# A planner that counts packets and holds transfers back: one change to the plan of the DMA queue

## The chip, the core and the metric

The kernel runs on one core of a Trainium2 chip. A core has five engines with an instruction queue each: PE (TensorE, matrix products), DVE (VectorE), ACT (ScalarE), POOL (GpSimd) and SP (SyncE). In this kernel SP does nothing but issue transfers between the chip's memory (DRAM in the code) and the core's own memory; 16 DMA engines then move the bytes. Each queue is worked off strictly in its order: an instruction that waits holds up everything behind it on its engine. The metric is the device time of one execution in microseconds (us); less is better.

## The reference, cut to what matters

One layer of a hybrid encoder, for 2048 positions of width 1024. The input is normalised and projected once, and the columns of the projection go to two groups of heads:

```python
h = rms_norm(x, norm_w[l])
proj = h @ w_in[l]
dn = gated_deltanet_bidir(dn_q, dn_k, dn_v, dn_beta, dn_decay, ...)   # 4 heads of 128, both directions
dn = rms_norm(dn, dn_out_norm_w[l]) * silu(dn_z)
sw = windowed_gqa_with_sinks(sw_q, sw_k, sw_v, ...)                   # 8 query heads of 64, |i-j| <= 128
sw = sw * silu(sw_z)
x = x + concatenate([dn, sw]) @ w_out[l]
```

The first group (DeltaNet) applies a short convolution to q, k and v. It then cuts the positions into chunks, and for each chunk solves a small triangular system. Finally it carries a state from chunk to chunk, once forward and once backward. The second group is attention in blocks of 128 queries over a band of 384 keys.

## The kernel before, in words

**Stages.** Phase A works in two halves of 1024 positions. It loads x and the weights, splits both into a high and a low part, and does three matmuls for each product (lines 190 to 192 and 201 to 203). It runs the convolution (line 241) and the windowed attention in between. What later stages need goes out to DRAM: k and q of a head to `kq_d`, v to `v_d`, the gates to `zdn_d` and `zsw_d`, the attention's result to `mix_sw`.

Phase B takes the four DeltaNet heads in turn. For each head, `pre_front` loads four pieces of k, q (tile `kq`, line 654) and v (`vt`, 656) and a decay table (`dc`, 664), and writes the triangular matrices to DRAM (`m_d`, 708). `solve` reads their diagonal blocks back (`X` and `L`, 731 and 732), inverts them on DVE in 31 steps, and writes the result to DRAM (`x_d`, 746). `invert` reads it back in another layout (`xc`, 757) and builds the whole inverses with matmuls on PE (772). `scan` then goes through 16 chunks in both directions; each step loads `kqc` (810), which has four buffers for a direction, and ends in `post` (mix of the normalised output with the gate, 864 to 882).

While one head is in its scan, the next one is in `pre_front`, `solve` and `invert`. Between them lie 32 units of the output projection of the attention part (`sw_units`, lines 568 to 604). Each unit loads `mxs` (587) and often `zcs` (590), splits it (594, 595), loads a piece of x (`xrs`, 597), multiplies (600 to 602), adds on DVE (603) and stores a part of the sum (`part`, 604). At the end `out_dn` adds the DeltaNet part and writes the output (554 to 566).

**What sets the order.** No order is written out by hand. `set_order` (line 936) takes all instructions, works out which depends on which, gives each a duration, and plans them against a model of the five engines. `plan` (line 1161) is a list scheduler: the engine that can start first takes, of the instructions whose inputs are there, the one with the highest priority. It is run forward and backward in turn, 12 rounds (line 1224), each pass giving the other its priorities; the best of the last five forward plans is kept. The chosen order is then fixed for each of the five queues (line 1235). So the planned times never reach the chip: only the five orders do.

**The model of a transfer.** SP is busy for 500 ns with each issue (line 1084). The moving is done by one resource, `bus`, that takes one transfer after the other; `move[k]` (line 1114) is how long it holds it, and a transfer's data counts as there after its start on the bus plus the issue, a lag of 2400 ns (line 929) and its `move`. Before the change `move` is the bytes over 300 bytes per ns, whatever their layout, and SP may issue the next transfer however many are waiting for `bus` (lines 1205 to 1207). The first 14 loads have a fixed order, and no other transfer is issued before the last of them (lines 1069 to 1078).

Of the kernel before, what the change touches and what calls it, by code (L numbers as in the profile page):

```python
# [13 lines left out]
DRAM = bass.MemoryType.DRAM  # L14
# [921 lines left out]
def set_order(tc):  # L936


    insts, boundaries = [], []
# [7 lines left out]
    tiles = {x.name: x for x in tc.tiles}  # L947

    def aps(l):
        return [a.bass_ap for a in l if hasattr(a, "bass_ap")]  # L950

    def size(a):
        r = 1
        for _, c in list(a.ap)[1:]:
            r *= c
        return r

    def box(a, shape):
        stride = [1] * len(shape)
        for d in range(len(shape) - 2, -1, -1):  # L960
            stride[d] = stride[d + 1] * shape[d + 1]
        lo, off = [], a.offset
        for s in stride:
            lo.append(off // s)
            off %= s
        hi = list(lo)
        for step, count in a.ap:
            if step > 0 and count > 1:
                d = next(d for d, s in enumerate(stride) if s <= step)
                hi[d] += -(-(count - 1) * step // stride[d])  # L970
        for d in range(len(shape) - 1, 0, -1):
            if hi[d] >= shape[d]:
                hi[d - 1] += hi[d] // shape[d]
                lo[d], hi[d] = 0, shape[d] - 1
        return lo, hi
# [13 lines left out]
    for k, (i, eng) in enumerate(insts):  # L989
        touched = [(a, False) for a in aps(i.ins)] + [(a, True) for a in aps(i.outs)]  # L990
        for a, w in touched:
            name = a.tensor.name
            if name not in tiles:
                continue
            x = tiles[name]
            psum = "PSUM" in str(x.space)
            b = box(a, list(x.shape))
            used.setdefault(name, []).append(k)
            past = hist.setdefault(name, [])
            for k2, e2, w2, b2 in past:  # L1000
                if (w or w2) and (
                    (psum and (e2 == "PE") != (eng == "PE"))
                    or all(p <= s and r <= q for p, q, r, s in list(zip(b[0], b[1], b2[0], b2[1]))[1:])
                ):
                    edge(k2, k, w2)
            if psum and eng != "PE" and past and past[-1][1] != "PE" and past[-1][0] != k:
                if past[-1][1] == eng:
                    started[past[-1][0]].append(k)
                else:
                    edge(past[-1][0], k)  # L1010
            past.append((k, eng, w, b))
# [34 lines left out]
    for x in sorted((x for x in tc.tiles if x.tag in home and x.name in used), key=lambda x: used[x.name][0]):  # L1046
        name, bufs = home[x.tag]
        users.setdefault(name, []).extend(used[x.name])
        k = used[x.name][0]
# [6 lines left out]
        r = ring.setdefault(x.tag, [])  # L1056
# [18 lines left out]
    for x in used:  # L1075
        k = used[x][0]
# [32 lines left out]
    move, late = [0.0] * total, [0.0] * total  # L1109
    nxt, prv = [[] for _ in range(total)], [[] for _ in range(total)]  # L1110
    for k in range(total):
        if eng[k] == "SP":
            a = aps(insts[k][0].outs)[0]
            move[k] = a.ap[0][1] * size(a) * 4 / 300
            spread = [x.ap[0][0] == 0 for x in aps(insts[k][0].ins)]
            late[k] = 2000 * any(spread)
        lag = LAG[eng[k]] + move[k] + late[k] if k < n else 0
        if eng[k] == "PE" and not insts[k][0].is_transpose and "float32r" not in str(insts[k][0].ins[0].dtype):
            lag += 40
        if eng[k] == "Activation" and len(aps(insts[k][0].outs)) > 1:  # L1120
            lag += 90
        for s in succ[k]:
            if eng[s] == eng[k] != "SP":
                nxt[k].append((s, SAME[eng[k]] * ((k, s) in wrote)))
            else:
                nxt[k].append((s, lag))
        for s in started[k] if k < n else ():
            nxt[k].append((s, None))
        for s, d in nxt[k]:
            prv[s].append((k, d))  # L1130
# [30 lines left out]
    def plan(order, forward):  # L1161
        to, back = (nxt, prv) if forward else (prv, nxt)
        left, at = [len(x) for x in back], [0.0] * total
        later, ready = {e: [] for e in ENGINES}, {e: [] for e in ENGINES}
        free, queue = dict.fromkeys(ENGINES, 0.0), {e: [] for e in ENGINES}
        begin, bus, held = [0.0] * total, 0.0, 0.0

        def release(k, t):
            todo = [(k, t)]
            while todo:  # L1170
                k, t = todo.pop()
                for s, d in to[k]:
                    if d is not None:
                        at[s] = max(at[s], t + dur[k] + slow[k] + d)
                    else:
                        at[s] = max(at[s], t if forward else t + dur[k] + slow[k] - dur[s] - slow[s])
                    left[s] -= 1
                    if left[s]:
                        continue
                    if eng[s]:  # L1180
                        heapq.heappush(later[eng[s]], (at[s], s))
                    else:
                        begin[s] = at[s]
                        todo.append((s, at[s]))

        for k in range(total):
            if not back[k] and eng[k]:
                heapq.heappush(later[eng[k]], (0.0, k))
            elif not back[k]:
                release(k, 0.0)  # L1190
        for _ in range(n):
            t, e = min(
                (free[e] if ready[e] else max(free[e], later[e][0][0]), e) for e in ENGINES if ready[e] or later[e]
            )
            while later[e] and later[e][0][0] <= t:
                k = heapq.heappop(later[e])[1]
                heapq.heappush(ready[e], (order[k], k))
            k = heapq.heappop(ready[e])[1]
            queue[e].append(k)
            if k in port:  # L1200
                t = max(t, held)
                held = t + dur[k]
            begin[k] = t
            free[e] = t + dur[k] + slow[k]
            if e == "SP":
                release(k, max(t, bus))
                bus = max(t, bus) + move[k]
            else:
                release(k, t)
        end = max(free.values())  # L1210
        return end, begin, queue
# [9 lines left out]
    for k in reversed(topo):  # L1221
        rank[k] = max([dur[k]] + [rank[s] if d is None else rank[s] + dur[k] + d for s, d in nxt[k]])
    now, best = plan([-r for r in rank], True), None
    for i in range(12):
        if i < 8:
            stretch(*now[1:])
        back = plan([-(b + d) for b, d in zip(now[1], dur)], False)
        now = plan([-(b + d) for b, d in zip(back[1], dur)], True)
        if i >= 7 and (best is None or now[0] < best[0]):
            best = now  # L1230
# [64 lines left out]
```

## Time and profile before

| | before |
|---|---|
| time, median of 3 runs | 1291.93 us (1291.03 to 1295.85) |
| the profiled execution's own time | 1291.8 us |
| its span, first to last instruction | 1290.0 us |
| mean granted TensorE clock | 0.988 |
| instructions | 22619 |
| bytes moved, mean rate | 205.36 MB, 159 GB/s |

The profile is of one execution. Its page gives busy times for each engine, the span in slices, the DMA queues, the chain of work that ended last (followed back from the last instruction, at each step to what released it), and the costliest groups of instructions. Further views of the trace give the busy time of each engine in chosen stretches, the transfers of a stretch with their median time from issue to landing, and the queue of one engine in order of time. "DMA share" is the mean busy share of the 16 DMA engines; slightly above 1 is possible, since packets are counted by the stretch in which they begin.

### The profile page before, as it was taken

How to read it: one execution, taken by the hardware profiler on the slowest of the kernel's cores; microseconds unless marked ns; L12 is line 12 of the kernel's file. 1: busy time of each engine (PE TensorE's matmuls, PEld its weight loads, DVE VectorE, ACT ScalarE, POOL GpSimd, SP SyncE). 2: the span in 40 equal slices, each digit the busy share in tenths (PEclk: the TensorE clock that was granted, in tenths of full speed). 3: DMA queues.
4: the chain of work that ended last, by engine and by line, in shares of the span. 5: the costliest groups of instructions: out<-in, count | busy, mean ns of one | idle time of the engine just before them, and what ended most of it. 6: DMA issues, size and time to landing. Idle time of an engine off the chain costs nothing.

```text
span 1290.0 us, 22619 instructions
## 1 busy us (share of the span) xinstructions
PE 1231.0 (95%) x7162; PEld 1058.8 (82%) x7162; DVE 903.9 (70%) x2266; ACT 718.4 (56%) x2121; POOL 509.8 (40%) x876
## 2 busy tenths in 40 slices
PE   6999989999999999999999997999799899999998
PEld 6998778888889998888888886788688689898876
DVE  4422388999975689999986474689579869656433
ACT  5422254776744577777664325768657845675310
POOL 2230053757612297665320104833582482640000
PEclk9999999999999999999999997999999999999999
DMA  7442243322544433422127736966965875644765
GB/s 260 148 131 84 84 163 121 116 83 90 156 149 145 127 104 103 150 90 75 71 93 234 219 100 204 254 176 200 282 162 174 267 204 172 196 152 133 253 236 207
DMA packets 225511, 205.36 MB, mean 159 GB/s; under 512 B 48496, under 2 KB 175088, under 8 KB 225392
## 3 DMA queue, kind: packets, MB, share of 16 engines
q1 hardware_dynamic: 225392, 203.92, 50.9%
q8 instruction: 57, 0.93, 0.3%
q14 instruction: 62, 0.51, 0.1%
HBM read 138.79 MB, written 65.08 MB: 158 GB/s over the span
## 4 chain that ended last, share of the span: by engine, by line
PE 68%; DVE 13%; issue 6%; DMA 6%; ACT 4%; POOL 3%; SPq 0%; DVEq 0%; POOLq 0%; ACTq 0%
PE pf_c L190 5%; PE pf_c L191 5%; PE pf_c L192 5%; PE pf_z L190 4%; PE pf_z L191 4%; PE pf_z L192 4%; PE pi L772 3%; PE pt L364 3%; DVE acc L241 2%; PE pq_q L201 2%; PE pq_q L202 2%; PE pq_q L203 2%; PE pcd L563 2%; PE pcd L564 2%; PE pcd L562 2%
## 5 line engine op out<-in xcount | busy, mean ns | idle before, releaser
L190 PE MATMUL pf_c<-xhi,wh_c 128*128 128x512 f32 x384 | 151.2, 406 | 3.2 <-DVE acc L241 3.2
L241 DVE SCALAR_TENSOR_TENSOR acc<-pf_c,cw,acc 128x512 f32<-128x512 f32 (+2 forms) x192 | 140.0, 742 | 17.0 <-ACT acc L237 16.1
L191 PE MATMUL pf_c<-xlo,wh_c 128*128 128x512 f32 x384 | 151.0, 404 | 0.0
L192 PE MATMUL pf_c<-xhi,wl_c 128*128 128x512 f32 x384 | 149.8, 404 | 0.0
L359 POOL TENSOR_SCALAR pr<-pr,st 128x384 f32<-128x384 f32 (+1 forms) x128 | 84.8, 679 | 73.2 <-DVE st L357 49.9
L192 PE MATMUL pf_z<-xhi,wl_z 128*128 128x512 f32 x256 | 90.8, 401 | 0.0
L191 PE MATMUL pf_z<-xlo,wh_z 128*128 128x512 f32 x256 | 90.8, 399 | 0.0
L190 PE MATMUL pf_z<-xhi,wh_z 128*128 128x512 f32 x256 | 89.8, 400 | 0.0
L190 PEld LDWEIGHTS pf_c<-xhi,wh_c 128*128 128x128 f32 x384 | 72.7, 190 | 16.9 <-DVE acc L241 3.6
L350 ACT ACTIVATE pr<-pr,st 128x384 f32<-128x384 f32 (+1 forms) x128 | 76.1, 596 | 16.4 <-DVE st L349 14.3
L191 PEld LDWEIGHTS pf_c<-xlo,wh_c 128*128 128x128 f32 x384 | 72.6, 190 | 13.7
L192 PEld LDWEIGHTS pf_c<-xhi,wl_c 128*128 128x128 f32 x384 | 72.4, 189 | 13.8
L368 ACT ACTIVATE ph<-pt 128x512 fp32r<-128x512 f32 x92 | 53.7, 594 | 46.9 <-PE pt L364 41.3
L345 DVE CUSTOM_DVE_ANT_0 pr<-s,mask,sink 128x384 f32<-128x384 f32 (+1 forms) x128 | 72.7, 592 | 4.8 <-PE pt L364 2.5
L364 PE MATMUL pt<-ident,pr 128*128 128x128 f32 x368 | 71.5, 275 | 1.5 <-POOL pr L359 1.4
L826 ACT ACTIVATE yk<-py,ck 128x128 f32<-128x128 f32 x120 | 43.8, 365 | 48.4 <-PE py L821 47.2
L684 POOL TENSOR_TENSOR nk<-ssk,pw 128x4 f32<-128x4 f32 x16 | 16.9, 1059 | 131.0 <-DVE ssk L683 95.0
L703 DVE SCALAR_TENSOR_TENSOR ma<-gh,bp,dc 128x256 f32<-128x256 f32 x128 | 55.0, 476 | 19.4 <-PE gh L694 15.2
L369 DVE TENSOR_TENSOR pl<-pt,ph 128x512 fp32r<-128x512 f32 x92 | 62.0, 683 | 6.9 <-ACT ph L368 6.6
L364 PEld LDWEIGHTS pt<-ident,pr 128*128 128x128 f32 x368 | 48.1, 140 | 16.8 <-POOL pr L359 4.1
L202 PE MATMUL pq_q<-wh_q,xlo 128*128 128x256 f32 x256 | 61.5, 283 | 0.0
L201 PE MATMUL pq_q<-wh_q,xhi 128*128 128x256 f32 x256 | 61.1, 285 | 0.0
(253 smaller groups left out, 3798.4 us busy)
## 6 DMA issues: line engine op xcount, KB each, us to landing
kqc<-kq_d SPq DMA_DIRECT2D x120, 128.0 KB, 2.9
ws_c<-wt SPq DMA_DIRECT2D x48, 256.0 KB, 3.4
xr<-x SPq DMA_DIRECT2D x16, 512.0 KB, 5.3
ws_z<-wt SPq DMA_DIRECT2D x32, 256.0 KB, 3.6
kq<-kq_d SPq DMA_DIRECT2D x16, 512.0 KB, 5.4
m_d<-ma SPq DMA_DIRECT2D x32, 256.0 KB, 5.2
mxs<-mix_sw SPq DMA_DIRECT2D x32, 256.0 KB, 3.6
xrs<-x SPq DMA_DIRECT2D x32, 256.0 KB, 3.5
```

The source lines that it names most:

```text
L190: T.matmul(ps, hi[:, k, cs], xhi[b][:, k], start=(k == 0), stop=False)
L191: T.matmul(ps, hi[:, k, cs], xlo[b][:, k], start=False, stop=False)
L192: T.matmul(ps, lo[:, k, cs], xhi[b][:, k], start=False, stop=(k == KC - 1))
L201: T.matmul(ps[:, :n], xh, hi[:, k, :n], start=(k == 0), stop=False)
L202: T.matmul(ps[:, :n], xl, hi[:, k, :n], start=False, stop=False)
L241: V.scalar_tensor_tensor(av, ps[:, lo:], cw[:, i, k : k + 1], av, ALU.mult, ALU.add)
L345: V.tensor_tensor_reduce(pr[j][:, :n], ps[:, :n], mask[:, lo * P : hi * P], 1.0, sink[:, hh : hh + 1], ALU.add, ALU.max, accum_out=mx[:, j ...
L350: A.activation(pr[j][:, :n], pr[j][:, :n], AF.Exp, bias=nm[:, j : j + 1], accum_out=den[:, j : j + 1])
L359: G.tensor_scalar(pr[j][:, :n], pr[j][:, :n], den[:, j : j + 1], 1.0, ALU.mult, ALU.mult)
L364: T.transpose(pt[:, j], pr[j][:, (kb - lo) * P : (kb - lo + 1) * P], ident)
L369: V.tensor_tensor(pl, ptf, ph.bitcast(F32), ALU.subtract)
L703: V.scalar_tensor_tensor(ma[d, c4][:, c], gh[:, k], bp[:, d, cc : cc + 1], gms[d][:, c : c + 1].to_broadcast([P, 2, P]), ALU.mult, ALU.mult,)
```

## The change

Only the planner's model of a transfer is edited. The instructions, tiles and transfers are those of before; the order in each of the five queues is planned anew.

```diff
+    def run(a):
+        inside = a.tensor.name in tiles and "DRAM" not in str(tiles[a.tensor.name].space)
+        r = 1
+        for step, c in reversed(list(a.ap)[1:] if inside else list(a.ap)):
+            if step != r:
+                break
+            r *= c
+        return min(r, 2048)
+
...
         if eng[k] == "SP":
             a = aps(insts[k][0].outs)[0]
-            move[k] = a.ap[0][1] * size(a) * 4 / 300
+            count = a.ap[0][1] * size(a)
+            piece = min(run(x) for x in aps(insts[k][0].ins) + [a])
+            move[k] = count / piece * (8 + 0.148 * piece) / 16
...
             if e == "SP":
                 release(k, max(t, bus))
                 bus = max(t, bus) + move[k]
+                free[e] = max(free[e], bus - 1000)
             else:
```

`run` gives how many numbers lie in one unbroken piece of a transfer's source or target (within a partition, for a tile of the core's memory), at most 2048. The smaller of the two is the transfer's packet. `move` becomes the number of packets times 8 ns plus 0.148 ns for each 4-byte number, divided by 16 engines. The last added line keeps SP from its next issue until no more than 1000 ns of planned moving is waiting. Both hold in the forward and in the backward passes.

## The prediction

> **What bounds the kernel now.** The page comes first: busy times, the DMA queue, then the shares of the chain that ended last.
>
> ```profile
> PE 1231.0 (95%) x7162; PEld 1058.8 (82%) x7162; DVE 903.9 (70%) x2266; ACT 718.4 (56%) x2121; POOL 509.8 (40%) x876
> q1 hardware_dynamic: 225392, 203.92, 50.9%
> PE 68%; DVE 13%; issue 6%; DMA 6%; ACT 4%; POOL 3%; SPq 0%; DVEq 0%; POOLq 0%; ACTq 0%
> ```
>
> PE is the bound: 1231.0 of 1290.0 us. A new order of the same instructions can only win back idle time, 1290.0 - 1231.0 = 59.0 us, or lose more. DMA engines are half busy on average, but an average over stages hides where they are full. So next I read the busy times by stage, and then by the stretches where DMA fills up (engines in the order PE, PEld, DVE, ACT, POOL, then clock, DMA share, GB/s).
>
> ```profile
> 0.00:50.00 50.00, 38.56 (x267) 36.39 (x268) 25.59 (x42) 28.06 (x61) 15.06 (x38) 0.97 0.72 242
> 50.00:750.00 700.00, 692.21 (x3805) 589.38 (x3804) 515.85 (x1211) 397.11 (x965) 290.98 (x433) 1.00 0.39 122
> 750.00:1195.00 445.00, 410.23 (x2703) 360.99 (x2702) 327.44 (x956) 277.31 (x1055) 202.12 (x405) 0.97 0.65 193
> 1195.00:1290.00 95.00, 90.02 (x394) 72.02 (x392) 35.03 (x60) 15.95 (x43) 1.64 (x1) 1.00 0.68 232
> ```
>
> ```profile
> 785.00:815.00 30.00, 21.50 (x102) 16.79 (x101) 16.21 (x39) 20.55 (x93) 19.05 (x38) 0.72 0.92 262
> 835.00:850.00 15.00, 12.76 (x91) 11.54 (x90) 8.27 (x20) 11.48 (x39) 11.26 (x20) 1.00 0.90 243
> 890.00:930.00 40.00, 30.81 (x180) 24.74 (x179) 31.35 (x95) 28.56 (x124) 19.30 (x28) 0.96 0.87 256
> 1000.00:1050.00 50.00, 43.70 (x262) 36.02 (x261) 36.12 (x107) 35.49 (x147) 29.90 (x63) 0.97 0.88 254
> sum 135.00, PE 108.77 PEld 89.08 DVE 91.94 ACT 96.07 POOL 79.51; mean PE 27.19 PEld 22.27 DVE 22.99 ACT 24.02 POOL 19.88
> ```
>
> PE's idle time is 11.4 us in the opening, 7.8 us in the 700 us of the rest of phase A, 34.8 us in the scans, 5.0 us at the end. Of the 34.8, 135.00 - 108.77 = 26.2 us lie in four stretches in which the DMA share is 0.87 to 0.92. That is where an order of transfers can matter. Little of this idle time names DMA directly, though. In the list of waits the one wait of PE for a transfer in phase B is this:
>
> ```profile
> PE tr L674 <- DMA kq<-kq_d: 1.6, 1, 1.6
> PE tro L878 <- ACT oacc L875: 6.4, 4, 3.9
> ```
>
> The second row is why: PE mostly waits for other engines. The link to DMA is one step further back, in the chain of work in order of time (start, us, what):
>
> ```profile
> 911.26 6.80 DMA x_d<-X
> ...
> 922.67 4.65 DMA xc<-x_d
> ...
> 933.78 5.85 DMA xrs<-x
> ...
> 939.66 0.04 DVE xrs L603
> ...
> 940.26 0.35 DVE r L814
> ...
> 940.66 0.49 PE py L821 x2
> ```
>
> A load of x (`xrs`) arrives, DVE adds it, and only then does DVE reach the scan's `r`, for which PE waits. A late transfer of a filling unit stops the scan through DVE's fixed order.
>
> **The change, part by part.** It adds and removes no instruction on any queue. It does two things to the plan.
>
> *The count.* For 512-byte packets (128 numbers: kqc, dc, m_d, zcs) the old price of one is 128 x 4 / 300 x 16 = 27.3 ns, the new one 8 + 0.148 x 128 = 26.9 ns: no change. For 2 KB packets (mxs, xrs, vt, kq) it falls from 109.2 to 83.8 ns, so 256 KB goes from 874 to 670 ns of bus. For 128-byte packets (X, L, xc) it rises from 6.8 to 12.7 ns, X and L from 874 to 1630 ns each. Over the whole queue the old plan books 203.92 MB / 300 = 680 us; the new one, from the row of q1, (225392 x 8 + 50.98 million x 0.148) / 16 = 584 us. The profile has 50.9% of 1290.0 = 657 us. The new sum is 11% too short, the old one 3.5% too long. By itself I price the count at nothing; bounds are in the rival below.
>
> *The limit.* SP now stands still in the plan while over 1 us of moving waits. With 500 ns for an issue and 670 ns for a 256 KB transfer, the backlog grows by 170 ns each, by 840 ns for kq (1340 ns). So it acts only in bursts. In the full stretches there are bursts. Here are medians from issue to landing, over the whole run, then for 890 to 940 us:
>
> ```profile
> kqc<-kq_d SPq DMA_DIRECT2D x120, 128.0 KB, 2.9
> ...
> mxs<-mix_sw SPq DMA_DIRECT2D x32, 256.0 KB, 3.6
> xrs<-x SPq DMA_DIRECT2D x32, 256.0 KB, 3.5
> ...
> x_d<-X SPq DMA_DIRECT2D x4, 512.0 KB, 4.4
> ```
>
> ```profile
> q1 hardware_dynamic: 20104, 13.10, 88.9%
> ...
> kqc<-kq_d SPq DMA_DIRECT2D x8, 128.0 KB, 5.3
> ...
> mxs<-mix_sw SPq DMA_DIRECT2D x3, 256.0 KB, 5.6
> x_d<-X SPq DMA_DIRECT2D x1, 512.0 KB, 6.8
> ...
> xrs<-x SPq DMA_DIRECT2D x2, 256.0 KB, 5.1
> ```
>
> The excess is queueing: x_d 2.4, mxs 2.0, xrs 1.6, kqc 2.4 us. With at most 1 us allowed to wait, a newcomer finds between 0 and 1 us, 0.5 on average (an estimate). Kept excess 0.5, so x_d gains 1.9, mxs 1.5, xrs 1.1: 4.5 us for this stretch. These three I count one after the other: x_d opens the round trip to the next head's inverses, mxs feeds PE in the meantime, and xrs stands ahead of the scan on DVE, as the chain shows. kqc I count as nothing, covered by its four buffers; without that cover it would add up to 1.9. The same for the other two stretches, first 785 to 815, then 1000 to 1050:
>
> ```profile
> q1 hardware_dynamic: 10994, 7.82, 91.4%
> ...
> mxs<-mix_sw SPq DMA_DIRECT2D x2, 256.0 KB, 5.9
> ...
> xrs<-x SPq DMA_DIRECT2D x1, 256.0 KB, 5.2
> ```
>
> ```profile
> q1 hardware_dynamic: 20750, 12.62, 87.0%
> ...
> mxs<-mix_sw SPq DMA_DIRECT2D x5, 256.0 KB, 4.4
> xrs<-x SPq DMA_DIRECT2D x5, 256.0 KB, 3.9
> ...
> x_d<-X SPq DMA_DIRECT2D x1, 512.0 KB, 5.4
> ```
>
> At 785: mxs 2.3 - 0.5 = 1.8, xrs 1.7 - 0.5 = 1.2, together 3.0. At 1000: x_d 1.0 - 0.5 = 0.5, mxs 0.8 - 0.5 = 0.3, xrs nothing, together 0.8. The sum is 4.5 + 3.0 + 0.8 = 8.3 us. Bounds: with the full 1 us left waiting, 3.0 + 2.0 + 0 = 5.0; with all excess gone, 6.0 + 4.0 + 2.2 = 12.2. What is late next is PE's wait for ACT and DVE in the same places, so nothing beyond the 26.2 us of idle time can follow.
>
> *The rest of the run.* In the opening, the first 14 loads keep their order, so I put nothing. In the rest of phase A a DMA share of 0.39 leaves little to hold back and PE idles 7.8 us: nothing, between a gain of 4 and a loss of 4 (half its idle time either way, a guess at what a fresh order does). At the end, with no other stage beside it, nothing.
>
> The profiled execution is 1291.8 us (span 1290.0 and 1.8 around it), 0.1 below the median. **1291.8 - 8.3 = 1283.5 us.**
>
> One row speaks against holding back: SP's own queue shows that the chip already does.
>
> ```profile
> 936.55 3.80 SPq L732 DMA_DIRECT2D L<-m_d  x1
> ```
>
> An issue planned at 500 ns took 3.80 us while the queue was full, so a plan that stops SP there is nearer the truth. The Trainium skill, "DMA: Bandwidth & Descriptors", section "Rules for kernel authors", says the opposite of holding back: issue a transfer early and wait for it late, so that its fixed cost is hidden. No run shown here tells the two apart. By that rule the time would be that of the first rival, 1300.2 us; by the rows, 1283.5.
>
> **The rivals.**
>
> *Held back and priced too low: slower.* With the limit, a transfer that nobody needs soon is issued only when the planned bus is nearly free, and the planned bus is too fast. From the three q1 rows the new plan books 23.6, 40.3 and 39.6 us of bus in the three stretches (8 ns for a packet, 0.148 for each number, over 16); the old books 26.1, 43.7 and 42.1; the shares of 30, 50 and 50 us measure 27.4, 44.4 and 43.5. The shortfall grows from 3.4 to 11.8 us, by 8.4. Its place is the pieces that feed `pre_front` (kq, vt, dc), each with other engines' fixed orders behind it. If those arrive later by the shortfall, with nothing left between landing and use, the time is 1291.8 + 8.4 = 1300.2 us, 1303.6 with all 11.8. It decides once the planned slack of a load is below about 4 us, one stretch's shortfall. For it: the count is too low. Against it: old orders had landings of 5 to 7 us where the plan had about 4, and PE named DMA for 1.6 us only.
>
> *The limit hardly acts: same.* If SP is held by waits for producers more than by moving, its order stays, and only small re-orderings remain: 1291.8 us, within 4 us. For it: bursts must be long to build up 1 us. Against it: the full shares and the 3.80 us issue.
>
> *More than the excess.* If a better order of transfers lets the scans run on, up to all 26.2 us: 1265.6. Against it: most waits there name ACT and DVE.
>
> **How the numbers follow.** The forecast (1279.6 to 1286.8) has 0.40, the slower rival 0.34, no effect 0.19, the large gain 0.07. A measurement can tell about 0.5% from no change, 6.5 us: below 1285.5 is faster, above 1298.4 slower. Of the forecast 0.33 lies below 1285.5 and 0.07 above; of the slower rival 0.31 lies above 1298.4 and 0.03 below; no effect gives 0.15 same and 0.02 to each side. So faster 0.33 + 0.07 + 0.02 = 0.42, same 0.07 + 0.03 + 0.15 = 0.25, slower 0.33. The range takes in the forecast, part of the large gain, and the slower rival with its whole shortfall: 1272 to 1304. The forecast's own range is 1279.6 to 1286.8.
>
> **What would show it.** Right: landings of x_d, mxs and xrs in the full stretches near 4.5 us, and idle time of PE there down from 26.2 to about 18 us. The slower rival: new waits of PE, ACT or POOL for kq, vt or dc, or for what these feed, at the start of a head. No effect: the same medians. I am wrong altogether if phase A, which I put at nothing, moves by more than 4 us, or if the landings shorten and PE's idle time stays.

## The result and the profile after

The changed kernel takes 1299.67 us (median of 5 runs, 1298.75 to 1302.58) against 1294.21 us for before in the same comparison (5 runs, 1291.03 to 1295.85). The ratio is 1.0052 with an interval of 1.0038 to 1.0066: slower by half a per cent, where 0.6% faster was forecast. The profiled execution took 1299.67 us (span 1297.9). The one of before, 1291.8, lies at the low end of its runs, so the two profiles differ by 7.9 us where the medians differ by 5.5; a few us in a comparison of single profiles are the execution, not the kernel.

The page of after, the same three lines as for before:

```profile
PE 1234.0 (95%) x7162; PEld 1059.9 (82%) x7162; DVE 901.4 (69%) x2266; ACT 718.2 (55%) x2121; POOL 509.0 (39%) x876
q1 hardware_dynamic: 225392, 203.92, 50.7%
PE 72%; DMA 8%; DVE 6%; ACT 5%; POOL 5%; issue 3%; SPq 1%; DVEq 0%; POOLq 0%; ACTq 0%
```

Packets and bytes are the same to the last one, and so are the instruction counts of the engines. What grew is PE's idle time, from 59.0 to 1297.9 - 1234.0 = 63.9 us, and its busy time, by 3.0 us. The latter can be the clock: the opening below ran at 0.93 of it, against 0.97. By stage (engines PE, PEld, DVE, ACT, POOL, then clock, DMA share, GB/s):

```profile
0.00:50.00 50.00, 37.51 (x258) 35.46 (x258) 24.49 (x41) 28.94 (x61) 14.86 (x36) 0.93 0.70 242
50.00:750.00 700.00, 694.27 (x3813) 588.84 (x3813) 514.74 (x1219) 394.69 (x964) 293.79 (x436) 1.00 0.39 122
750.00:1195.00 445.00, 406.04 (x2662) 358.31 (x2660) 320.35 (x930) 273.24 (x1043) 198.73 (x403) 0.97 0.64 187
1195.00:1297.90 102.90, 96.14 (x432) 77.31 (x432) 41.78 (x79) 21.34 (x54) 1.64 (x1) 1.00 0.70 238
```

Fixed stretches mix what was late with what was slow. Two marks cut the run at nearly the same work in every kernel: the last matmul of the gates' projection (`pf_z`, end of phase A's products) and the first of the last output stage (`pcd`). At the first mark PE has started 4217 or 4218 of its 7162 matmuls in every kernel of this document. The view of a tile gives the first and last start of its instructions. Before:

```profile
L192 PE MATMUL pf_z<-xhi,wl_z x256: 387/393/585, 91.9 to 783.2; 128*128 128x512 f32 x128
```

```profile
L562 PE MATMUL pcd<-wohd,mhd x128: 387/389/496, 1194.9 to 1285.5; 128*128 128x512 f32 x128
```

After:

```profile
L192 PE MATMUL pf_z<-xhi,wl_z x256: 388/393/581, 93.7 to 783.2; 128*128 128x512 f32 x128
```

```profile
L562 PE MATMUL pcd<-wohd,mhd x128: 387/389/497, 1202.6 to 1293.4; 128*128 128x512 f32 x128
```

Both reach the first mark at 783.2 us. From there to the second, which I call the scans, before needs 1194.9 - 783.2 = 411.7 us, after 1202.6 - 783.2 = 419.4. The last stage is as long in both (90.6 and 90.8). **The whole loss between these two profiles, 7.7 us, is in the scans.** Here are the engines between the marks, before and then after:

```profile
783.20:1194.90 411.70, 376.93 (x2555) 333.80 (x2553) 301.88 (x887) 270.85 (x1036) 201.22 (x403) 0.97 0.68 201
```

```profile
783.20:1202.60 419.40, 378.43 (x2550) 335.97 (x2548) 303.07 (x886) 271.57 (x1035) 198.73 (x403) 0.97 0.68 197
```

PE's idle time there grows from 411.70 - 376.93 = 34.8 to 419.40 - 378.43 = 41.0 us, so 6.2 of the 7.7 us are waits. A third mark says when they come: PE's first product in the scan of the third head (`py` from `vs`), before and after:

```profile
L821 PE MATMUL py<-vs,ma x4: 272/274/275, 1042.2 to 1045.1; 128*128 128x128 f32 x4
```

```profile
L821 PE MATMUL py<-vs,ma x4: 273/275/275, 1048.4 to 1049.9; 128*128 128x128 f32 x4
```

From the first mark that is 259.0 and 265.2 us: 6.2 us are lost by then, while the first two heads are in their scans and the next ones are prepared.

Now the rows on which the forecast rested. The four full stretches of after:

```profile
785.00:815.00 30.00, 20.56 (x99) 17.13 (x98) 16.58 (x44) 21.75 (x96) 18.73 (x36) 0.77 0.94 269
835.00:850.00 15.00, 14.30 (x99) 12.70 (x98) 9.09 (x26) 12.09 (x40) 12.42 (x21) 1.00 0.75 185
890.00:930.00 40.00, 31.87 (x191) 26.00 (x190) 30.20 (x91) 28.40 (x125) 18.57 (x34) 0.96 0.90 260
1000.00:1050.00 50.00, 42.19 (x244) 34.15 (x245) 35.37 (x106) 34.01 (x148) 26.03 (x56) 0.97 0.83 237
sum 135.00, PE 108.92 PEld 89.97 DVE 91.23 ACT 96.24 POOL 75.75; mean PE 27.23 PEld 22.49 DVE 22.81 ACT 24.06 POOL 18.94
```

Idle time of PE there is 135.00 - 108.92 = 26.1 us; it was 26.2. So the idle time that the scans gained shows outside the four stretches: 41.0 - 26.1 = 14.9 us, where it was 34.8 - 26.2 = 8.6 (as far as fixed stretches can tell, since the work shifts by some us). And the transfers of 890 to 940 us, median us from issue to landing in the last column:

```profile
q1 hardware_dynamic: 20083, 12.75, 90.7%
...
kqc<-kq_d SPq DMA_DIRECT2D x8, 128.0 KB, 5.5
...
x_d<-X SPq DMA_DIRECT2D x1, 512.0 KB, 6.7
mxs<-mix_sw SPq DMA_DIRECT2D x2, 256.0 KB, 3.8
xrs<-x SPq DMA_DIRECT2D x2, 256.0 KB, 5.6
```

Only mxs lands sooner (5.6 before). x_d stays (6.8), xrs and kqc are later (5.1 and 5.3). The other two stretches, 785 to 815 and 1000 to 1050:

```profile
mxs<-mix_sw SPq DMA_DIRECT2D x2, 256.0 KB, 5.2
...
xrs<-x SPq DMA_DIRECT2D x1, 256.0 KB, 7.3
```

```profile
xrs<-x SPq DMA_DIRECT2D x4, 256.0 KB, 3.7
...
mxs<-mix_sw SPq DMA_DIRECT2D x3, 256.0 KB, 3.6
...
x_d<-X SPq DMA_DIRECT2D x1, 512.0 KB, 5.4
```

All eight changes together: (-0.1 - 1.8 + 0.5) + (-0.7 + 2.1) + (-0.2 - 0.8 + 0.0) = -1.0 us, where 8.3 were forecast. In SP's queue in order of time an issue still stands behind the one before it:

```profile
935.41 4.44 SPq L732 DMA_DIRECT2D L<-m_d  x1
```

It took 4.44 us, right behind the load of `X` (3.80 in the same place before). For the first head, where the same load came 4 us after that of `X`, it took 0.59 us in before. Nothing of the limit is in the code that reaches the chip: the five orders are, and the limit has shaped them and nothing else.

### The profile page after: what moved, and what is told of

Its sections match the earlier page's. It is cut to its first block, busy times and chain, and to the rows that moved or that the text cites. A ratio compares the mean times of both kernels' runs of the same rounds, so it can differ in the third digit from the quotient of the medians.

```text
span 1297.9 us, 22582 instructions
## 1 busy us (share of the span) xinstructions
PE 1234.0 (95%) x7162; PEld 1059.9 (82%) x7162; DVE 901.4 (69%) x2266; ACT 718.2 (55%) x2121; POOL 509.0 (39%) x876
## 3 DMA queue, kind: packets, MB, share of 16 engines
q1 hardware_dynamic: 225392, 203.92, 50.7%
## 4 chain that ended last, share of the span: by engine, by line
PE 72%; DMA 8%; DVE 6%; ACT 5%; POOL 5%; issue 3%; SPq 1%; DVEq 0%; POOLq 0%; ACTq 0%
PE pf_c L190 6%; PE pf_c L192 5%; PE pf_c L191 5%; PE pf_z L190 4%; PE pf_z L191 4%; PE pf_z L192 4%; PE pi L772 3%; PE pt L364 3%; PE pq_q L201 2%; PE pq_q L202 2%; PE pq_q L203 2%; PE pcd L562 2%; PE pcd L563 2%; PE pcd L564 2%; DMA kq<-kq_d 2%
## 5 line engine op out<-in xcount | busy, mean ns | idle before, releaser
L241 DVE SCALAR_TENSOR_TENSOR acc<-pf_c,cw,acc 128x512 f32<-128x512 f32 (+1 forms) x192 | 140.5, 742 | 10.1 <-ACT acc L237 7.8
L190 PE MATMUL pf_z<-xhi,wh_z 128*128 128x512 f32 x256 | 87.1, 402 | 0.0
L191 PE MATMUL pf_z<-xlo,wh_z 128*128 128x512 f32 x256 | 86.0, 398 | 0.0
L192 PE MATMUL pf_z<-xhi,wl_z 128*128 128x512 f32 x256 | 85.9, 399 | 0.0
## 6 DMA issues: line engine op xcount, KB each, us to landing
ws_c<-wt SPq DMA_DIRECT2D x48, 256.0 KB, 3.2
ws_z<-wt SPq DMA_DIRECT2D x32, 256.0 KB, 3.8
m_d<-ma SPq DMA_DIRECT2D x32, 256.0 KB, 5.1
mxs<-mix_sw SPq DMA_DIRECT2D x32, 256.0 KB, 3.3
xrs<-x SPq DMA_DIRECT2D x32, 256.0 KB, 3.5
```

The costliest lines, as they stand in the source:

```text
L190: T.matmul(ps, hi[:, k, cs], xhi[b][:, k], start=(k == 0), stop=False)
L191: T.matmul(ps, hi[:, k, cs], xlo[b][:, k], start=False, stop=False)
L192: T.matmul(ps, lo[:, k, cs], xhi[b][:, k], start=False, stop=(k == KC - 1))
L241: V.scalar_tensor_tensor(av, ps[:, lo:], cw[:, i, k : k + 1], av, ALU.mult, ALU.add)
```

## The experiments

Theories at the start: **A**, the first rival, the new price of a transfer is too low. **B**, the limit holds loads back too long. **C**, any new plan of so many instructions lands somewhere within a few tenths of a per cent, whatever the edit says. Later came **D**: the limit gains in phase A and loses in the scans. Each result is the ratio to before, with its interval. The table at the end of this section gives the two parts of each profiled execution, cut at the marks above.

**The two parts of the change alone, and two controls.**

```diff
# count_only: the changed kernel without
-                free[e] = max(free[e], bus - 1000)
# limit_only: the changed kernel with the old price
-            move[k] = count / piece * (8 + 0.148 * piece) / 16
+            move[k] = count * 4 / 300
# rate_301, rate_299: the kernel before with
-            move[k] = a.ap[0][1] * size(a) * 4 / 300
+            move[k] = a.ap[0][1] * size(a) * 4 / 301     # and 299
```

> The new price of a transfer (packets counted) without the limit on SP; before as the base is 1294. Theory A (the new price books too little bus, 584 us against a measured 657, and so the plan counts on loads too early): the loss is the price's, so slower by 0.4 to 0.8%, 1299 to 1304 us, with the loss again at the changes of head. Theory B (the limit holds loads back too long): without the limit the loss is gone, 1289 to 1295 us. Theory C (any new plan of these 22,600 instructions lands somewhere within about 1% of the old, whatever the edit says): anything from 1288 to 1306 us, and the stages in which it gains or loses are not those of the full change.

> The limit of 1000 ns on SP with the old price (bytes over 300). Theory A: the old price books 680 us, more than is measured, so nothing is counted on too early and the limit is free to help or to do nothing: 1283 to 1294 us. Theory B: the old price is higher for most transfers, so the limit acts more often, and the loss is as large as that of the full change or larger: 1300 to 1306 us. Theory C: anything from 1288 to 1306 us, without the pattern of the full change.

> The kernel before with 301 instead of 300 bytes per ns in the planner, no other edit: 0.3% less for the moving of each transfer, a few ns. Theories A and B: nothing that matters is changed, so 1291 to 1297 us (within 0.2% of before). Theory C: the plan is as new as that of the full change, so it differs from before by 0.2 to 0.8%, to either side.

> The kernel before with 299 instead of 300 bytes per ns in the planner, no other edit. Theories A and B: 1291 to 1297 us, as with 301. Theory C: differs from before by 0.2 to 0.8%, to either side, and not by the mirror image of what 301 gives.

Measured: count_only 1.0003 (0.9990 to 1.0017), limit_only 0.9997 (0.9979 to 1.0015), rate_301 1.0009 (0.9996 to 1.0022), rate_299 0.9966 (0.9953 to 0.9979). Neither part alone costs anything, so A and B fall as they stood. And a constant changed by 0.3% moves the time by 0.34% in one case. Compared place by place in the traces, by operation, tiles and shapes, rate_301 has another matmul than before in 4416 of the 7162 places of PE's order and limit_only in 3893: in these plans a constant moved by 0.3% changes the order as much as the limit does. C was the likeliest by now, but the profiles of limit_only and of the full change agreed in one respect. Here is limit_only at the two marks:

```profile
L192 PE MATMUL pf_z<-xhi,wl_z x256: 387/393/585, 89.2 to 779.1; 128*128 128x512 f32 x128
```

```profile
L562 PE MATMUL pcd<-wohd,mhd x128: 388/389/501, 1199.8 to 1290.5; 128*128 128x512 f32 x128
```

It is 4.1 us ahead at the first mark, and needs 420.7 us for the scans, 9.0 more than before. Its total is even because a gain and a loss cancel.

**The limit in one phase only, and the full change with a hair's difference.**

```diff
# lim_A and lim_B: limit_only, with the limit by phase
+    cut = min(used[x][0] for x in used if x.startswith("kq0_"))
...
-                free[e] = max(free[e], bus - 1000)
+                if k < cut:        # lim_B: k >= cut
+                    free[e] = max(free[e], bus - 1000)
# lim_990: the changed kernel with bus - 990; num_1485: with 0.1485 * piece
```

> Old price, with the limit on SP only for the transfers of phase A (those recorded before the first load of pre_front); before as the base is 1295. Both plans with the limit (the full change and the limit alone) were 3 to 5 us ahead of before at 400 us and lost 8 to 9 us between 784 us and the end, the plans without it lost nothing there. Theory D (the limit helps in phase A and hurts in the scans): ahead by 4 us at 784 us and no loss behind it, so 1288 to 1292 us, faster by 0.2 to 0.5%. Theory C (only a new plan's luck): the gain at 784 us is anywhere from -6 to +5 us and the total anywhere from 1288 to 1303 us.

> Old price, with the limit only for the transfers of phase B. Theory D: even with before at 784 us, and 7 to 10 us lost by the end of the scans, most of it in the scan of the second head, so 1301 to 1305 us. Theory C: anywhere from 1288 to 1303 us, and where it loses or gains is another place than in the full change.

> The full change with 990 instead of 1000 ns in the limit, nothing else: the same idea in every respect, with a plan that differs in part. Theory A, B and D (the loss comes from what the change says): 1299 to 1303 us, as the full change. Theory C: the full change was an unlucky plan, and this one lies elsewhere by 0.2 to 0.6%, more likely lower: 1290 to 1299 us.

> The full change with 0.1485 instead of 0.148 ns for a number, nothing else. Theory A, B and D: 1299 to 1303 us, as the full change. Theory C: elsewhere by 0.2 to 0.6%, more likely lower: 1290 to 1299 us.

Measured: lim_A 0.9963 (0.9943 to 0.9983), lim_B 1.0044 (1.0031 to 1.0058), lim_990 1.0052 (1.0035 to 1.0069), num_1485 1.0043 (1.0028 to 1.0058). All four times came as D has it. The place that was named for lim_B did not: of its 7.4 us more in the scans than before, 4.8 are lost before the second head's scan begins. C, for the full change, falls: two neighbours, whose orders of PE differ from its own in 1510 and 3451 places, lose as much. The marks of lim_A:

```profile
L192 PE MATMUL pf_z<-xhi,wl_z x256: 387/393/585, 89.1 to 779.1; 128*128 128x512 f32 x128
```

```profile
L562 PE MATMUL pcd<-wohd,mhd x128: 388/389/501, 1189.3 to 1279.9; 128*128 128x512 f32 x128
```

and of lim_B:

```profile
L192 PE MATMUL pf_z<-xhi,wl_z x256: 387/393/585, 92.2 to 785.0; 128*128 128x512 f32 x128
```

```profile
L562 PE MATMUL pcd<-wohd,mhd x128: 388/389/501, 1204.1 to 1294.7; 128*128 128x512 f32 x128
```

lim_A is as far ahead at 779.1 as limit_only and needs 410.2 us for the scans; lim_B gains nothing in phase A and needs 419.1. And -0.37% + 0.44% is about the 0 of limit_only.

**The parts put together, and SP's order by itself.**

```diff
# count_lim_A: the changed kernel with the limit for k < cut only
# lim_A_301: lim_A with 301 instead of 300
# sp_of_lim: the plan of lim_B is made; its order of SP is kept as a chain,
# and the other queues are planned anew without the limit (search() is the 12 rounds)
+    lim = True
+    for x, y in zip(*(lambda q: (q, q[1:]))(search()[2]["SP"])):
+        nxt[x].append((y, None))
+        prv[y].append((x, None))
+    slow[:] = [0.0] * total
+    lim = not lim
+    best = search()
# sp_plain: the same with lim = False both times
```

> The full change with its limit only for the transfers of phase A; before as the base is 1295. If the loss of the full change is its limit in phase B (theory D), it is gone: phase A as in the full change, phase B as with the count alone, so 1290 to 1296 us, faster by up to 0.3% or even. If the loss comes from the two parts of the change together, wherever the limit acts, 1299 to 1303 us.

> A control: the plan of before is made, its order of SP is kept as a fixed chain, and the other four queues are planned anew by the model of before. SP's order is that of before, the others differ. By the scatter of plans seen so far (-0.34 to +0.09%) 1290 to 1298 us; above 1300 would say that planning under a fixed order of SP costs something by itself.

> As the control, but the order of SP is that of the plan with the limit in phase B; the other four queues are planned for it by the model of before, without the limit. Theory D1 (it is SP's order by itself that costs on the chip): slower than the control by 0.4 to 0.7%, 5 to 9 us, lost in the scan of the second head. Theory D2 (the order of SP is harmless, and the orders that came out for the other engines beside it cost the time): within 0.2% of the control.

> The limit in phase A alone, with 301 instead of 300 bytes per ns. If the gain of the limit in phase A is real, faster again by 0.2 to 0.5%, 1288 to 1292 us, with 3 to 5 us gained by 400 us; if it was one plan's luck, 1292 to 1298 us.

Measured: count_lim_A 0.9994 (0.9976 to 1.0013), sp_plain 1.0021 (1.0007 to 1.0035), sp_of_lim 1.0058 (1.0038 to 1.0079), lim_A_301 0.9949 (0.9932 to 0.9967). The full change without its limit in phase B is even: that limit is its loss. The gain in phase A came again in a second plan. The order of SP from the plan with the limit costs 0.37% more than that of before when the other queues are planned in the same way for both. That lies between what the two theories asked for (0.4 to 0.7%, and within 0.2%), and it is hardly more than the 0.34% by which a constant alone moved the time. The scans of these two profiles are 418.2 and 417.4 us long. So that the harm travels with SP's order is suggested, not shown. sp_plain even speaks against SP's order as the only place: it has that of before, to the last transfer by name, and in its profile (an execution 2.9 us above its median) the scans are 5.7 us longer. So the other four orders can move them about as far.

**What in that order.** In the plans with the limit in phase B, between 840 and 1060 us, mxs, xrs and part stand 0.9 to 2.2 places earlier on average than in before (zcs within 0.8 to either side), and kqc 1.0 to 1.6 places later.

```diff
# units_back: sp_of_lim, with each transfer of mxs, zcs, xrs and part in SP's chain
# moved up to two places later, as far as it passes nothing that depends on it
# and no other transfer of these
# units_fwd: sp_plain, with the same transfers up to two places earlier
# lim_B_fwd, lim_B_bwd: lim_B, with the limit in one direction of the passes
-                if k >= cut:
+                if forward and k >= cut:        # lim_B_bwd: not forward
```

> The order of SP of sp_of_lim (limit in phase B, 0.58% slower than before), in which each transfer of the filling units (mxs, zcs, xrs and the store of part) is moved up to two places later where nothing needs it first; the other queues are planned anew without the limit. In the five plans with the limit in phase B these transfers stood 1 to 2 places earlier than in before, between 840 and 1060 us, and the scan's kqc 1.0 to 1.6 places later. Theory U (the units' transfers ahead of the others are what costs): back to the control sp_plain, 0.1 to 0.3% slower than before, 1296 to 1299 us. Theory V (another part of the new order costs): stays at 0.4 to 0.7%, 1300 to 1304 us.

> The mirror image: the order of SP of before (as in the control sp_plain, 0.21% slower than before), with the filling units' transfers moved up to two places earlier. Theory U: slower than the control by 0.3 to 0.5%, 1300 to 1304 us. Theory V: within 0.2% of the control, 1295 to 1300 us.

> Limit in phase B, old price, but only in the forward passes, which make the orders; the backward passes, which give the priorities, run without it. If the loss is made when SP stands still going forward and picks from those ready later (theory F), slower by 0.35 to 0.55%, 1299 to 1302 us. If it is made in the priorities (theory P), within the scatter of plans, 1290 to 1297 us.

> The counterpart: the limit in phase B only in the backward passes. Theory P (the priorities are spoilt): slower by 0.35 to 0.55%, 1299 to 1302 us. Theory F: within the scatter of plans, 1290 to 1297 us.

Measured: units_back 1.0083 (1.0068 to 1.0097), units_fwd 1.0075 (1.0056 to 1.0094), lim_B_fwd 0.9999 (0.9982 to 1.0016), lim_B_bwd 1.0019 (1.0006 to 1.0032). Theory F falls, and P isn't borne out by +0.19%.

Theory U is left undecided. units_fwd came slow, as U has it, and even beyond it. units_back should have come back to sp_plain and is slower still. But its profile shows that most of the extra time isn't where U spoke of it. Its last `py` of the scans starts here:

```profile
L821 PE MATMUL py<-r,ma x240: 270/275/377, 837.2 to 1199.7; 128*128 128x128 f32 x120
```

That is 1199.7 - 788.9 = 410.8 us after the first mark, where sp_of_lim needs 417.0, sp_plain 416.2 and before 410.2. Then 10.4 us pass until the output stage, where those three take 1.2 to 1.5. PE does little in them:

```profile
1200.00:1205.00 5.00, 0.93 (x5) 0.59 (x4) 1.71 (x7) 3.60 (x19) 0.60 (x1) 1.00 0.72 245
1205.00:1210.00 5.00, 2.53 (x8) 1.46 (x8) 1.89 (x4) 4.09 (x13) 1.04 (x1) 0.56 0.62 196
```

Its longest wait there, 5.6 us, is for ACT's `oacc` (line 875), the mix after the last scan. So this run lost at the end what it had won back in the scans, and it can't refute U. Against U stands lim_B_fwd, which has these transfers early too (mxs by 2.3 places, kqc 1.6 later) and loses nothing: their place by itself isn't enough. The last two runs asked P again:

```diff
# lim_A_Bfwd: limit_only, without the limit in the backward passes over phase B
+                if forward or k < cut:
# lim_B_bwd_301: lim_B_bwd with 301 instead of 300
```

> Old price; the limit everywhere but in the backward passes over phase B. It takes from the limit what gained (phase A, -0.37 and -0.51% in two plans) and what did no harm (forward passes over phase B, even). If the harm sits in the backward passes, faster by 0.2 to 0.5%, 1288 to 1292 us; if it needs only the limit's presence in phase B, 1295 to 1300 us, as the limit alone and slower.

> The limit only in the backward passes over phase B, with 301 instead of 300 bytes per ns: a second plan of the same idea as lim_B_bwd (+0.19%). If the priorities are where the harm is made, slower again by 0.1 to 0.5%, 1296 to 1301 us; if the +0.19% was that plan's luck, anywhere from 1288 to 1297 us.

Measured: lim_A_Bfwd 0.9968 (0.9952 to 0.9985), lim_B_bwd_301 0.9981 (0.9968 to 0.9995). The backward passes alone don't harm either: +0.19 and -0.19% are two plans' scatter.

All kernels, by what they have of the limit (times of a single profiled execution, us; an execution can differ by some us from another of the same kernel):

| limit | kernel | ratio | to the first mark | scans |
|---|---|---|---|---|
| none | before | 1 | 783.2 | 411.7 |
| none | rate_299, rate_301 | 0.9966, 1.0009 | 784.0, 785.7 | 406.1, 410.6 |
| none | count_only | 1.0003 | 788.9 | 408.3 |
| phase A | lim_A, lim_A_301 | 0.9963, 0.9949 | 779.1, 779.2 | 410.2, 415.3 |
| phase A | count_lim_A | 0.9994 | 785.6 | 407.6 |
| phase A, B forward | lim_A_Bfwd | 0.9968 | 780.8 | 413.1 |
| phase B forward | lim_B_fwd | 0.9999 | 782.9 | 411.3 |
| phase B backward | lim_B_bwd, lim_B_bwd_301 | 1.0019, 0.9981 | 785.6, 784.9 | 415.7, 411.9 |
| phase B both ways | lim_B | 1.0044 | 785.0 | 419.1 |
| phase A, B both ways | limit_only | 0.9997 | 779.1 | 420.7 |
| phase A, B both ways | after | 1.0052 | 783.2 | 419.4 |
| phase A, B both ways | lim_990, num_1485 | 1.0052, 1.0043 | 786.4, 789.1 | 416.7, 417.8 |
| SP's order fixed | sp_plain, sp_of_lim | 1.0021, 1.0058 | 787.6, 787.0 | 417.4, 418.2 |
| SP's order fixed | units_back, units_fwd | 1.0083, 1.0075 | 788.9, 787.5 | 421.2, 416.7 |

Of the plans made freely, the five with the limit in both passes over phase B need 416.7 to 420.7 us for the scans, and the eleven others 406.1 to 415.7. The two groups are only 1.0 us apart, in single executions. The five are also fewer than they look: lim_B and limit_only have the same order of SP in the scans, by the names of the transfers, and lim_990 is close kin to after. Those are three plans or so; among the eleven, too, lim_A shares SP's order in the scans with before but for two places, and lim_A_Bfwd with lim_B_fwd. The medians say more. Three pairs differ by the limit over phase B alone, and it costs each time: limit_only against lim_A 0.34%, lim_B against before 0.44%, after against count_lim_A 0.58%. The third mark points the same way: the five come to it 263.7 to 267.8 us after the first, ten of the eleven after 256.0 to 262.3, and lim_A_301 after 264.6. So that the limit in both directions costs there is seen in every plan tried; by what, is open. sp_plain and units_fwd, whose chain of SP comes from before, reach such lengths without the limit. It could be one bad arrangement that these plans have in common.

The fastest kernels are lim_A_301 and lim_A, 0.51 and 0.37% faster than before, and their intervals exclude 1. Both beat the changed kernel too. How much of that the limit earned isn't settled by the totals, since rate_299 has no limit and gains 0.34%. The gain at the first mark is better shown, though by single executions: with the old price, or 1 byte per ns beside it, the four plans with the limit in phase A reach it at 779.1 to 780.8 us, the seven without it at 782.9 to 785.7. Some of it lies in the opening. This is lim_A:

```profile
0.00:50.00 50.00, 40.00 (x290) 37.66 (x291) 27.34 (x43) 28.47 (x60) 17.04 (x36) 1.00 0.72 238
```

PE starts 290 matmuls there at full clock (288 in lim_A_301 and limit_only), against 267 at 0.97 in before.

## Why the prediction was wrong

**The step that failed** is the one that turned the limit into shorter landings: "With at most 1 us allowed to wait, a newcomer finds between 0 and 1 us, 0.5 on average (an estimate). Kept excess 0.5, so x_d gains 1.9, mxs 1.5, xrs 1.1". The wait is allowed or forbidden in the plan; on the chip, as the description of the kernel says, only the order arrives. The DMA engines were as full as before, with a share of 0.90 at 890 to 930 us against 0.87, and the eight landings gave back 1.0 us of the 8.3. PE's idle time in the four stretches moved by 0.1. To shorten a queue, an order has to put fewer transfers ahead of a wanted one at the time when it is wanted, and of that the prediction had looked at nothing.

**A term that wasn't in the sum** holds most of the loss. The prediction went through the four stretches, the opening, phase A and the end. The rest of the scans it left out, and with it what a new order does there: PE's idle time in the scans but outside the four stretches went from 8.6 to 14.9 us.

**The count priced at nothing**: right as a total, 1.0003 for the count alone. In its one profile 5.7 us are lost in phase A and 3.4 gained in the scans, so "nothing" is a sum of two, each within what a new plan does by itself.

**The rest of the run priced at nothing**: right for the change as a total (783.2 us to the first mark in both, 90.6 and 90.8 at the end), but again by two parts that cancel. The limit gains in phase A with the old price, where I saw no burst to act on: 4.1 us in lim_A, just over the bound of 4 that I had set. In the changed kernel the new price lost it: 788.9 for the count alone, 783.2 with the limit.

**The first rival** named the time, 1300.2 against 1299.67, by luck and not by the cause. Its mechanism was a price that is too low. Yet the low price alone costs nothing, and the old, high price loses as much in the scans (lim_B, 1.0044). Its sign was there, in the row of PE's waits for kq of after:

```profile
PE tr L674 <- DMA kq<-kq_d: 5.3, 4, 3.1
```

That is 5.3 us where before had 1.6. But limit_only, with the longest scans of these plans, has this:

```profile
PE tr L674 <- DMA kq<-kq_d: 1.3, 2, 1.1
```

A sign that comes and goes with plans that lose alike is no cause. The rule of the Trainium skill that was weighed, in "DMA: Bandwidth & Descriptors", section "Rules for kernel authors", is to issue a transfer early and wait for it late. These runs don't decide on it: in the two rows above PE waits longer for kq in one plan and shorter in the other, and both lose.

**What I left out** is C as a term. Nowhere did the prediction ask how far a plan moves when nothing of substance is changed. It gave "small re-orderings" to the rival without effect, within 4 us; rate_299 moved by 4.4 (0.34% of 1295).

**What stays open**: which instructions, in SP's order or in the other four, cost the 5 to 9 us of the scans, and why it takes the limit in both directions. That the filling units' transfers stand earlier isn't enough by itself (lim_B_fwd); whether it takes part isn't settled.

## What to carry to other kernels

An edit to a planner's model reaches the chip as an order and in no other way: don't price a limit in the model as if the hardware kept it. Before reading meaning into a change of some tenths of a per cent, plan again with a constant moved by 0.3%, more than once; and when a total is even, cut the run at marks of equal work, since a gain in one phase and a loss in another can hide behind it. An edit that helps one phase and harms another is best applied by phase.

## What the runs showed of the hardware

The count's coefficients put the whole queue at 584 us, and the DMA engines were busy for 50.7% of 1297.9 = 658 us: the packets of this kernel take an eighth longer than the formula says. It fits the typical packet and not the mean. In the trace of before the median packet of 512 bytes took 27 ns and that of 2 KB 84 ns, as the formula has it, and the means are 28.7 and 97.7 ns.

Where PE stands for a while in these traces, its clock is mostly lower right behind it. Cut into stretches of 5 us from 700 to 1190 us, all the profiled executions together have 44 in which PE is busy for less than 2.3 us; 42 of them are followed by one with a mean granted clock of 0.50 to 0.90, and two by full clock. At the change from the second head to the third, lim_B has this:

```profile
1030.00:1035.00 5.00, 2.16 (x9) 1.20 (x7) 3.60 (x10) 2.29 (x12) 1.24 (x1) 0.95 0.66 163
1035.00:1040.00 5.00, 4.11 (x11) 3.21 (x12) 1.54 (x6) 2.45 (x8) 4.39 (x16) 0.50 0.79 217
```

PE is busy for 2.16 of 5 us, and in the next 5 us the granted clock is 0.50. In before the same is seen in the first of the forecast's stretches: PE is busy for 2.04 us at 785 to 790, and the clock is 0.50 from 790 to 805. So a pause of PE can cost twice, once as a wait and once in the products behind it; no run here separates the two.
